# A hybrid attention layer on one NeuronCore: 166 more entries in a list that reorders the planned instructions

## The chip, the cores and the metric

The kernel runs on one core of a Trainium2 chip. Its engines, as the profile names them, are PE (TensorE, matmuls and transposes; its weight loads have a row PEld), DVE (VectorE), ACT (ScalarE), POOL (GpSimd) and SP (SyncE, which here issues every DMA). Each engine works through its own instructions in order; an instruction waits where it needs data that another engine or a transfer has not delivered. The metric is the device time of one execution in microseconds.

## What is computed

One layer of a streaming encoder, for 1024 prompt tokens and 32 sample tokens with shared weights, all in float32:

```python
def rmsnorm(x, g):
    x32 = x.astype(jnp.float32)
    y = x32 * lax.rsqrt(jnp.mean(x32 * x32, axis=-1, keepdims=True) + RMS_EPS)
    return (y * g.astype(jnp.float32)).astype(x.dtype)

def in_proj(h, g_pre, w_in):                     # w_in: 1024 x 4096
    u = rmsnorm(h, g_pre) @ w_in
    qa, ka, va, ga, qb, kb, vb, gb = jnp.split(u, SPLIT_IDX, axis=-1)
    ...

def band_attention(q, k, v, q_pos, k_pos, bias_table):     # "A", 8 heads x 64
    s = jnp.einsum('bqhd,bkhd->bhqk', q, k).astype(jnp.float32) * ATTN_SCALE
    rel = jnp.clip(k_pos[None, :] - q_pos[:, None], -REL_CLIP, REL_CLIP) + REL_CLIP
    s = s + bias_table[:, rel].astype(jnp.float32)[None]
    ...                                          # own 64-frame chunk and the 8 before it
    w = jax.nn.softmax(s, axis=-1).astype(v.dtype)
    return jnp.einsum('bhqk,bkhd->bqhd', w, v)

def stick_breaking(q, k, v, q_pos, k_pos):       # "B", 8 heads x 64
    z = jnp.einsum('bqhd,bkhd->bhqk', q, k).astype(jnp.float32) * ATTN_SCALE
    causal = (k_pos[None, :] < q_pos[:, None])[None, None]
    log_beta = jax.nn.log_sigmoid(z)
    log_1m = jnp.where(causal, jax.nn.log_sigmoid(-z), 0.0)
    after = lax.cumsum(log_1m, axis=3, reverse=True) - log_1m
    w = jnp.where(causal, jnp.exp(log_beta + after), 0.0).astype(v.dtype)
    return jnp.einsum('bhqk,bkhd->bqhd', w, v)

def finish(h, oa, ga, ob, gb, w_out, g_post, p, w_ple, w_ple_gate):
    y = jnp.concatenate([oa * jax.nn.silu(ga), ob * jax.nn.silu(gb)], axis=-1) @ w_out
    h = h + rmsnorm(y, g_post)
    return h + jax.nn.sigmoid(h @ w_ple_gate) * (p @ w_ple)
```

The sample tokens attend to cached keys and values of 512 earlier positions too. Outputs are the two results, and the new keys and values of both groups.

## The kernel before

**Arithmetic.** Every float32 operand of a matmul is split into a high part (`...h`, a cast to fp32r) and a low part (`...l`, the rest), and a product is three or four matmuls of such parts. The casts are ACT's, the subtractions DVE's or POOL's.

**Stages.** At the start, the small product `p @ w_ple` (class `Ple`: tiles `pp`, `wpr`, `php`, `ple`) fills PE while x is normed and transposed (`ptx`, `hnh`, `hnl`). Then the projection columns are made in pairs of heads (`mm_kA`, `mm_qA`, ...; weights `wr` split into `wh`, `wl`), woven (`weave`, L1352) with the attention of the pair before: pairs A0, B0, A1, B1, ... each of two heads. `A20` is pair 2 of A, head 0. Gates `gA` and `gB` follow, and at the end the products with `w_out` and `w_ple_gate`, seven block products each instead of eight, which need sums of weight blocks.

**Attention of one head.** `scores` (L915) makes eight query blocks of scores (`SA`, `SB`). For B, ACT takes the sigmoid into `om`, DVE scans along it, and POOL subtracts neighbours into `be`, the weights. For A, DVE adds the bias (`om`), and ACT takes the exponential into `be`. `weights_t` (L963) turns the weights: early blocks by PE transposes (`ptwA`, `ptwB`), blocks 4 to 7 by a DVE transpose in 32 x 32 squares and a round trip through DRAM, a store `swapA<-om` and a load `be<-swapA`. The result is split into `wTh` and `wTl`, and `values` (L1011) multiplies by the values `v2A`, `v2B` into `PVA`, `PVB`, which become `otA`, `otB` and are stored to `o_dr`. The values themselves take such a round trip too (`stvA<-swapA`, then `vtA` and `v2A`, `values_out`, L766). `om` and `be` are rings (`Arena`, L232): a new tile waits until all readers of the old one in its place are done, the stores among them.

**Weight sums.** `sum_weights` (L1390) loads four quarter blocks of `w_out` (tiles `oB`) or the gate's weight (`gB`), subtracts and adds halves of them on POOL, and stores the sums (`sum_dro`, `sum_drg`) for the last stage. They are spread over the attention of pairs A0, B0 and A2, B2.

**What sets the order.** No operation is issued as it is written. A `Recorder` collects 9,413 operations, 7,493 of them instructions and the rest (`CTL`) allocations of tiles. `order` (L402) plans them with a list scheduler and its own table of costs, improves the plan in 42 passes, and hands the best plan to `settle` (L421), which applies the list `MOVES` (L44) to it. `emit` (L531) then issues them in that order, all from L541, so each line of the profile has L541 and tiles tell the operations apart. The order in which an engine meets its instructions is this list, and SP's DMAs are part of it.

An entry `(i, j)` takes the operation at place i and puts it at place j, which is earlier. What it depends on between j and i goes ahead of it in the old order; on every engine but its own the order stays.

```python
        for i, j in MOVES:
            x = ops[i]
            need, engines, ahead, behind = set(x.after), {x.eng}, [], []
            for o in reversed(ops[j:i]):
                if o in need or (o.eng in engines and o.eng != x.eng):
                    assert o.eng != x.eng
                    ahead.append(o)
                    need |= o.after
                    if o.eng != "CTL":
                        engines.add(o.eng)
                else:
                    behind.append(o)
            ops[j:i + 1] = ahead[::-1] + [x] + behind[::-1]
```

Entries are applied one after another, so a later entry's places are those of the list that the earlier ones have left.

Of the kernel before, what the change touches and what calls it, by code (L numbers as in the profile page):

```python
# [57 lines left out]
    (5444, 5437), (6840, 6823), (5445, 5438), (6861, 6825), (696, 695), (2421, 2418), (2244, 2243), (6823, 6819), (4946, 4929), (1132, 1128),  # L58
    (4715, 4714), (1118, 1108), (2021, 1989), (1063, 1055), (725, 713), (748, 726), (1008, 1002), (2176, 2169), (3344, 3337), (2855, 2845), (3213, 3209),
    (331, 323), (1566, 1563), (1011, 1003), (2520, 2512), (6405, 6400), (8654, 8642), (6230, 6225), (6755, 6742), (3470, 3468), (3081, 3057),  # L60
    (7388, 7378), (7065, 7064), (2559, 2539), (4169, 4164), (4264, 4262), (3630, 3605), (3749, 3736), (6063, 6045),
)
PASSES, SPREAD = 42, 400

# [1912 lines left out]
```

## Time and profile before

| | before |
|---|---|
| time, median of 3 runs (range) | 772.1 us (771.61 to 772.69) |
| the profiled execution's own time | 772.48 us |
| its span, first to last instruction | 770.7 us |
| busy PE / DVE / ACT / POOL | 759.4 / 582.4 / 490.9 / 462.1 us |
| mean granted TensorE clock | 0.998 |
| HBM read / written | 107.62 / 65.30 MB, 224 GB/s over the span |

A row of the timeline gives start and length in us, engine, line, operation, output and inputs, shape and count, and in brackets how long the engine had been idle and what ended that. Rows that follow each other with the same names are merged (x2). A row of waits gives the total, the number and the longest of them. A row of the chain gives start, length and what ran, or what transfer was in flight. A row of windows gives the stretch, its length, the busy time of PE, PEld, DVE, ACT and POOL with their instructions, the granted clock, and the DMA engines' share and GB/s. PE's matmuls are pipelined, so its busy time overstates its work a little and hides the shortest waits.

### The profile page before, as it was taken

The numbers are of one execution on the slowest core, as the hardware profiler recorded it, in microseconds if no ns is written. First come the engines' busy times: TensorE is split into PE (matmuls) and PEld (weight loads), VectorE is DVE, ScalarE is ACT, GpSimd is POOL, SyncE is SP. The second block draws the span as 40 slices with busy tenths as digits, with TensorE's granted clock in tenths as the row PEclk, the third lists the DMA queues.
The fourth block names the chain that finished last, engine by engine and source line by source line (L and its number), as shares of the span: only waits on it lengthen the run. The fifth ranks groups of instructions, "written<-read, shape, count | busy, mean of one in ns | idle before, by whom it ended". The sixth has DMA issues, their size and how long they took to land.

```text
span 770.7 us, 13667 instructions
## 1 busy us (share of the span) xinstructions
PE 759.4 (99%) x4422; PEld 703.0 (91%) x4422; DVE 582.4 (76%) x1025; ACT 490.9 (64%) x995; POOL 462.1 (60%) x525
## 2 busy tenths in 40 slices
PE   8999999999999999999999999999999999999997
PEld 7999989999999999999999999999998877888786
DVE  6726879898799888978898899875563578587665
ACT  5736785666686657875677785633447967774551
POOL 6615637883344546556883336788453769898443
PEclk9999999999999999999999999999999999999999
DMA  8519999878976649999689779977687859879854
GB/s 277 169 36 271 264 279 301 233 232 266 250 218 190 184 130 276 260 273 294 183 247 289 180 209 294 273 221 207 197 276 252 281 155 337 274 251 337 272 184 137
DMA packets 184825, 182.24 MB, mean 236 GB/s; under 512 B 42177, under 2 KB 139497, under 8 KB 184754
## 3 DMA queue, kind: packets, MB, share of 16 engines
q1 hardware_dynamic: 184754, 181.37, 78.2%
q8 instruction: 35, 0.57, 0.3%
q14 instruction: 36, 0.29, 0.1%
HBM read 107.62 MB, written 65.30 MB: 224 GB/s over the span
## 4 chain that ended last, share of the span: by engine, by line
PE 88%; DMA 5%; ACT 3%; DVE 2%; SPq 1%; issue 0%; POOL 0%; ACTq 0%; DVEq 0%; POOLq 0%
PE mm_qA L541 6%; PE mm_vA L541 6%; PE mm_gA L541 6%; PE mm_gB L541 6%; PE mm_kA L541 6%; PE mm_kB L541 5%; PE mm_qB L541 4%; PE PVB L541 4%; PE SB L541 4%; PE mm_vB L541 3%; PE ple L541 3%; PE PVA L541 3%; PE SA L541 3%; PE g1P L541 3%; PE o3P L541 3%; PE o1P L541 3%
## 5 line engine op out<-in xcount | busy, mean ns | idle before, releaser
L541 POOL TENSOR_TENSOR be<-om 128x128 f32<-128x128 f32 (+7 forms) x64 | 80.4, 1261 | 52.3 <-DVE om L541 22.1
L541 DVE TENSOR_TENSOR_SCAN om<-om,SB 128x384 f32<-128x384 f32 (+5 forms) x96 | 94.4, 998 | 7.0 <-ACT om L541 4.1
L541 DVE TENSOR_TENSOR wTl<-be,wTh 128x640 fp32r<-128x640 f32 (+2 forms) x56 | 65.0, 1166 | 5.6 <-ACT wTh L541 5.5
L541 ACT ACTIVATE om<-SB 128x384 f32<-128x384 f32 (+5 forms) x96 | 44.6, 491 | 29.7 <-PE SB L541 15.3
L541 ACT ACTIVATE be<-om,statA 128x640 f32<-128x640 f32 (+3 forms) x64 | 46.4, 729 | 14.4 <-DVE statA L541 7.0
L541 DVE STREAM_TRANSPOSE om<-be 128x640 f32<-128x640 f32 (+2 forms) x56 | 49.6, 892 | 3.2 <-ACT be L541 2.4
L541 ACT CAST wTh<-be 128x640 fp32r<-128x640 f32 (+2 forms) x56 | 43.2, 774 | 11.0 <-DMA be<-swapA 7.8
L541 DVE CUSTOM_DVE_ANT_0 om<-SA,biasA 128x320 f32<-128x320 f32 (+3 forms) x64 | 29.9, 484 | 8.8 <-PE SA L541 7.5
L541 POOL TENSOR_TENSOR gB<-gB,gB 128x256 f32<-128x256 f32 x32 | 26.5, 848 | 12.6 <-DMA gB<-in_w_ple_gate_dram 6.3
L541 ACT CAST wTh<-ptwB 128x512 fp32r<-128x512 f32 (+3 forms) x48 | 22.0, 481 | 18.3 <-PE ptwB L541 12.7
L541 PE MATMUL SB<-klB,LB 128*128 128x384 f32 (+5 forms) x96 | 32.9, 347 | 0.0
L541 PE MATMUL SB<-kdB,LB 128*128 128x384 f32 (+5 forms) x96 | 32.6, 344 | 0.2 <-DVE om L541 0.2
L541 POOL TENSOR_TENSOR oB<-oB,oB 128x256 f32<-128x256 f32 x32 | 24.3, 780 | 12.4 <-DMA oB<-in_w_out_dram 10.5
L541 DVE TENSOR_TENSOR wTl<-ptwB,wTh 128x512 fp32r<-128x512 f32 (+3 forms) x48 | 25.6, 544 | 7.9 <-PE PVB L541 5.0
L541 DVE TENSOR_TENSOR SB<-SB,maskb 128x128 f32<-128x128 f32 x64 | 17.9, 289 | 15.9 <-PE SB L541 15.4
L541 POOL TENSOR_TENSOR sggA<-sggA,oggA 128x352 f32<-128x352 f32 x24 | 26.3, 1099 | 6.0 <-DVE sggA L541 5.5
L541 PE MATMUL SA<-klA,LA 128*128 128x320 f32 (+2 forms) x96 | 29.5, 318 | 0.0
L541 PE MATMUL SA<-kdA,LA 128*128 128x320 f32 (+2 forms) x96 | 29.3, 316 | 0.0
L541 POOL TENSOR_TENSOR klB<-stkB,kdB 64x1024 fp32r<-64x1024 f32 x8 | 19.2, 2400 | 9.6 <-ACT kdB L541 8.8
L541 POOL TENSOR_TENSOR klA<-stkA,kdA 64x1024 fp32r<-64x1024 f32 x8 | 20.1, 2510 | 7.8 <-ACT kdA L541 7.1
L541 PE MATMUL ptwB<-ident,be 128*128 128x128 f32 x144 | 21.8, 274 | 2.8 <-POOL be L541 1.4
L541 POOL TENSOR_TENSOR h<-h,x 128x512 f32<-128x512 f32 (+1 forms) x18 | 23.1, 1293 | 1.5 <-DVE h L541 1.4
(683 smaller groups left out, 2581.4 us busy)
## 6 DMA issues: line engine op xcount, KB each, us to landing
swapA<-om SPq DMA_DIRECT2D x32, 320.0 KB, 3.8
be<-swapA SPq DMA_DIRECT2D x32, 320.0 KB, 4.6
oB<-in_w_out_dram SPq DMA_DIRECT2D x16, 256.0 KB, 4.0
sum_dro<-oB SPq DMA_DIRECT2D x16, 256.0 KB, 4.1
gB<-in_w_ple_gate_dram SPq DMA_DIRECT2D x16, 256.0 KB, 4.1
sum_drg<-gB SPq DMA_DIRECT2D x16, 256.0 KB, 3.8
x<-in_x_prompt_dram SPq DMA_DIRECT2D x16, 256.0 KB, 5.0
turned<-hs SPq DMA_DIRECT2D x16, 256.0 KB, 5.1
```

Of the source, the lines that this page charges most:

```text
L541: getattr(getattr(tc.nc, o.what[0]), o.what[1])(*args, **kw)
```

## The change

The list `MOVES` gets 166 more entries behind the ones that are there. No operation is added, removed or resized, and nothing else differs. Followed through the order one after another, 94 of the entries move a DMA on SP, 25 an instruction of DVE, 22 of ACT, 14 of POOL and 11 of PE. 113 of them pass one instruction of their own engine, none more than six. In the end 120 of SP's 734 DMAs stand at another place of SP's order, by seven places at most; 50 of 925 on DVE, 38 of 892 on ACT, 27 of 520 on POOL and 25 of 4,422 on PE, by five places at most.

At the places that the prediction speaks of, in the times of the execution profiled before:

- SP at 1 us: the second half of `pp` and `grow` ahead of `wpr_0`. ACT: `php` ahead of the cast of `wpr_0`.
- SP at 93 to 103 us: the store `swapA<-om` of block 4 of A01 and four loads of biases change places with loads of weights `wr_qA` and key stores. At 106 to 108 us: the store of block 5 goes ahead of a load for the sums, the store of block 6 goes behind the store of block 7 and the first load `be<-swapA`. At 113 to 116 us: the load `oB` for the next sum goes behind the loads `be<-swapA` of blocks 6 and 7.
- POOL at 111 to 113 us: `be` of blocks 0 and 1 of B00 each go ahead of half a weight sum `oB`.
- ACT at 307 to 310 us: `be` of block 6 of A20, two casts `wTh` and the copy `otB` go ahead of the copies `vtA` and `v2A`.
- SP at 329 to 339 us: three loads of biases and a copy of keys go behind three loads of `gB`, a load of `wr_vA`, the load `be<-swapA` of block 4 of A21 and the stores of blocks 5 to 7.
- POOL at 344 to 348 us: `be` of block 3 of B20 goes ahead of two halves of sums `gB` and two memsets of `om`.

```diff
--- before.py
+++ after.py
@@ -58,7 +58,24 @@
     (5444, 5437), (6840, 6823), (5445, 5438), (6861, 6825), (696, 695), (2421, 2418), (2244, 2243), (6823, 6819), (4946, 4929), (1132, 1128),
     (4715, 4714), (1118, 1108), (2021, 1989), (1063, 1055), (725, 713), (748, 726), (1008, 1002), (2176, 2169), (3344, 3337), (2855, 2845), (3213, 3209),
     (331, 323), (1566, 1563), (1011, 1003), (2520, 2512), (6405, 6400), (8654, 8642), (6230, 6225), (6755, 6742), (3470, 3468), (3081, 3057),
-    (7388, 7378), (7065, 7064), (2559, 2539), (4169, 4164), (4264, 4262), (3630, 3605), (3749, 3736), (6063, 6045),
+    (7388, 7378), (7065, 7064), (2559, 2539), (4169, 4164), (4264, 4262), (3630, 3605), (3749, 3736), (6063, 6045), (88, 83), (3945, 3921), (4466, 4460),
+    (3937, 3924), (1278, 1246), (3960, 3949), (5541, 5537), (1034, 1024), (2066, 2050), (7065, 7064), (5596, 5593), (209, 204), (4474, 4471),
+    (4286, 4266), (6366, 6363), (6257, 6238), (6194, 6182), (4268, 4263), (4477, 4465), (1345, 1325), (2225, 2212), (5427, 5419), (275, 233),
+    (3839, 3821), (1149, 1130), (3968, 3912), (5511, 5492), (1114, 1090), (4612, 4606), (120, 118), (1290, 1284), (4727, 4715), (4465, 4449),
+    (1124, 1106), (6101, 6094), (4636, 4632), (4298, 4269), (2463, 2453), (6045, 6044), (6201, 6189), (1368, 1328), (3686, 3684), (94, 84), (4171, 4157),
+    (1394, 1370), (356, 322), (4268, 4267), (4262, 4261), (2538, 2522), (1365, 1358), (4784, 4775), (5957, 5950), (6332, 6307), (4305, 4271),
+    (4838, 4775), (2742, 2741), (9084, 9075), (4270, 4268), (4606, 4601), (6367, 6364), (4607, 4602), (2567, 2546), (6179, 6177), (4778, 4769),
+    (3913, 3912), (1388, 1370), (2521, 2513), (4454, 4437), (1398, 1389), (6570, 6554), (1405, 1390), (6039, 6028), (4142, 4136), (364, 339),
+    (4271, 4270), (4306, 4272), (1138, 1131), (6001, 5978), (4332, 4278), (5275, 5274), (1131, 1106), (4732, 4716), (6243, 6233), (3370, 3364),
+    (1091, 1072), (4269, 4267), (4514, 4504), (4285, 4271), (1115, 1073), (5135, 5118), (1116, 1114), (4499, 4476), (6183, 6182), (2424, 2419),
+    (4771, 4770), (1248, 1161), (4632, 4619), (1083, 1080), (4270, 4269), (946, 938), (6192, 6178), (4345, 4286), (1112, 1110), (3992, 3982),
+    (4206, 4201), (6655, 6654), (6656, 6653), (1114, 1111), (4033, 4023), (1132, 1117), (6639, 6630), (1324, 1303), (5581, 5579), (5995, 5989),
+    (6368, 6365), (5391, 5384), (4234, 4225), (4740, 4739), (5446, 5435), (5458, 5420), (4261, 4246), (4262, 4258), (5592, 5580), (2250, 2231),
+    (4498, 4492), (1312, 1303), (4644, 4620), (5019, 4980), (4213, 4180), (3822, 3821), (4268, 4261), (6031, 5989), (4354, 4291), (3950, 3927),
+    (1410, 1409), (2245, 2244), (1196, 1156), (2540, 2538), (323, 322), (1200, 1197), (4268, 4263), (4280, 4279), (243, 238), (324, 323), (6654, 6645),
+    (2368, 2357), (4195, 4180), (3046, 3020), (3720, 3714), (2029, 1989), (2332, 2317), (1133, 1118), (1107, 1072), (1575, 1574), (4046, 4035),
+    (2500, 2481), (7323, 7306), (1384, 1334), (4024, 4023), (2426, 2420), (3980, 3976), (3997, 3982), (754, 730), (1211, 1195), (4091, 4085),
+    (1143, 1118),
 )
 PASSES, SPREAD = 42, 400
```

## The prediction

> **What bounds the kernel now.** The page comes first: engine times, chain, then who waited for whom.
>
> ```profile
> span 770.7 us, 13667 instructions
> PE 759.4 (99%) x4422; PEld 703.0 (91%) x4422; DVE 582.4 (76%) x1025; ACT 490.9 (64%) x995; POOL 462.1 (60%) x525
> PEclk9999999999999999999999999999999999999999
> PE 88%; DMA 5%; ACT 3%; DVE 2%; SPq 1%; issue 0%; POOL 0%; ACTq 0%; DVEq 0%; POOLq 0%
> ```
>
> TensorE (PE) is the bound: busy for 759.4 of 770.7 us and 88% of the chain. No entry of the change adds, removes or resizes an instruction, so its busy work stays; all that a new order can win is the time in which PE stands. The view of waits, for PE alone, has it whole:
>
> ```profile
> PE ptwB L541 <- POOL be L541: 1.4, 1, 1.4
> PE ptwB L541 <- POOL sumsA L541: 1.4, 1, 1.4
> PE idle L541 <- DVE still L541: 1.3, 1, 1.3
> PE ptp L541 <- DMA pp<-in_p_prompt_dram: 0.7, 1, 0.7
> PE ptwA L541 <- DVE wTl L541: 0.6, 1, 0.6
> PE PVA L541 <- ACT wTh L541: 0.3, 1, 0.3
> PE SB L541 <- DVE om L541: 0.2, 1, 0.2
> ```
>
> Each row is one wait: its total equals its longest. The `idle` row lies ahead of the first matmul and no entry reaches it. The other six sum to 4.6 us, 3.9 without the start. That is about the ceiling of this change. So the question for each wait is whether the entries near it shorten it, and what comes late next. 108 of the 166 entries concern four stretches: 34 lie at 75 to 118 us, 14 at 296 to 315, 35 at 315 to 350, 25 at 350 to 455.
>
> **The change part by part.** *The wait at 112.0 us.* Timelines of PE, POOL and SP:
>
> ```profile
> 112.03 0.33 PE L541 MATMUL ptwB<-ident,be 128*128 128x128 f32 x1 [1.43 <-POOL be L541]
> 108.44 0.10 POOL L541 MEMSET om<- 128x1 f32 x1 [2.90 <-DVE otA L541]
> 110.90 0.72 POOL L541 TENSOR_TENSOR oB<-oB,oB 128x256 f32<-128x256 f32 x1 [2.36 <-DMA oB<-in_w_out_dram]
> 111.58 0.40 POOL L541 TENSOR_TENSOR be<-om 128x128 f32<-128x128 f32 x1
> 112.67 0.61 POOL L541 TENSOR_TENSOR be<-om 128x256 f32<-128x256 f32 x1
> ```
>
> PE transposes the 128x128 `be` that POOL makes at 111.58. POOL is in order, and ahead of that `be` stands half a weight sum (`oB`) that waits 2.36 us for a load. The entries put this `be` ahead of the sum, and the second `be` (112.67) ahead of the sum's other half. The first can then start when the memset of 108.44 is done, by 108.6: 3 us early, so the 1.4 goes. Next is the second `be`: it stands behind the first half sum, whose load holds the same turn on SP. It starts at 110.90 + 0.72 = 111.6 and ends at 112.2; PE, 1.4 us earlier, asks for it at about 112. I leave 0.2 and take -1.2; bounds 0 and -1.4.
>
> *The wait at 123.1 us* (the 0.3 of the waits), from the chain and PE's timeline:
>
> ```profile
> 116.56 5.70 DMA be<-swapA
> 123.06 0.68 PE L541 MATMUL PVA<-wTh,v2A 128*128 128x512 f32 x2 [0.25 <-ACT wTh L541]
> ```
>
> `wTh` needs a load of `be` that took 5.70 us. SP gets to it earlier: a load for the sums goes behind it. But PE comes 1.2 us earlier as well, and one of the four stores whose data this load reads back moves two places later. I cost it at nothing, bounds +1.2 (the load doesn't move, PE does) and -0.3.
>
> *The waits at 309.0 us.* ACT, DVE and PE:
>
> ```profile
> 307.18 1.05 ACT L541 COPY vtA<-stvA 128x1024 f32<-128x1024 f32 x1 [2.22 <-DMA stvA<-swapA]
> 308.14 0.53 ACT L541 CAST wTh<-ptwA 128x256 fp32r<-128x256 f32 x2
> 309.81 0.90 ACT L541 ACTIVATE be<-om,statA 128x640 f32<-128x640 f32 x1
> 308.70 0.29 DVE L541 TENSOR_TENSOR wTl<-ptwA,wTh 128x128 fp32r<-128x128 f32 x1 [1.29 <-ACT wTh L541]
> 309.05 0.55 PE L541 MATMUL ptwA<-ident,be 128*128 128x128 f32 x3 [0.58 <-DVE wTl L541]
> ```
>
> ACT stands 2.22 us before the `vtA` copy, which waits for a transfer, and behind it are two casts (0.53) that free the bank PE waits for. The entries put the `be` of 309.81 (0.90), both casts and then the `otB` copy ahead of `vtA`. ACT is free from 307.18 - 2.22 = 304.96; with 0.90 and 0.53 the casts end near 306.4 in place of 308.7, so DVE and PE have 2 us to spare: -0.6. `vtA` itself waits for its transfer as before. Next in line on ACT are the casts of the later banks, and these come sooner too, by the 0.90 taken out ahead of them. Bounds 0 and -0.6.
>
> *The waits at 344.6 and 348.2 us.* PE, DVE, POOL, the chain and SP:
>
> ```profile
> 344.61 0.45 PE L541 MATMUL SB<-kdB,LB 128*128 128x384 f32 x1 [0.24 <-DVE om L541]
> 348.22 0.55 PE L541 MATMUL ptwB<-ident,be 128*128 128x128 f32 x3 [1.37 <-POOL sumsA L541]
> 343.28 1.27 DVE L541 TENSOR_TENSOR_SCAN om<-om,SB 128x512 f32<-128x512 f32 x1
> 343.42 1.42 POOL L541 TENSOR_TENSOR gB<-gB,gB 128x256 f32<-128x256 f32 x2
> 346.36 0.13 POOL L541 MEMSET om<- 128x1 f32 x2 [1.52 <-DMA o_dr<-otA]
> 346.45 0.72 POOL L541 TENSOR_TENSOR gB<-gB,gB 128x256 f32<-128x256 f32 x1
> 347.14 1.02 POOL L541 TENSOR_TENSOR be<-om 128x512 f32<-128x512 f32 x1
> 335.84 5.92 DMA be<-swapA
> 337.08 1.53 SPq L541 DMA_DIRECT2D swapA<-om  x3
> ```
>
> PE waits for the 128x512 `be` of 347.14. Its input is ready when the scan ends, at 344.55; it stands behind two memsets, which wait 1.52 us for stores to land, and behind the second `gB` of the pair at 343.42 and the one at 346.45. The entries put it ahead of all of these, right behind the first `gB` of the pair, done by 344.2: it can start at 344.6 and end at 345.6, against 348.2. On SP the load at 335.84 and the first store at 337.08 go three places forward, past loads of biases and a copy of the next head's keys; with 1.53 / 3 = 0.5 us a place that is 1.5 us. The scan stands behind that load's consumers on DVE, so it comes earlier too, and with it the 0.2. I take -1.4 - 0.2 = -1.6; bounds 0 and -1.6. The biases moved back, seven places at most (some 3.5 us), belong to the sample attention of the next pair.
>
> *The start.* On SP the second half of `pp` and `grow` go ahead of the weights `wpr_0`; on ACT `php` goes ahead of their cast:
>
> ```profile
> 1.24 0.45 SPq L541 DMA_DIRECT2D wpr_0True<-in_w_ple_dram  x1
> 4.69 0.62 ACT L541 CAST wph0True<-wpr_0True 128x512 fp32r<-128x512 f32 x1 [2.69 <-DMA wpr_0True<-in_w_ple_dram]
> 5.82 1.12 PE L541 MATMUL ptp<-ident,pp 128*128 128x128 f32 x4 [0.73 <-DMA pp<-in_p_prompt_dram]
> 6.58 2.91 PE L541 MATMUL ple<-wph0True,php 128*128 128x512 f32 x6
> ```
>
> The two transfers trade landings: `pp` at about 4.7 in place of 5.8, `wpr_0` at 5.8 or later, then the cast of 0.62, and `ple` can begin at 6.45 or later against 6.58. The wait moves from `ptp` to `ple`: 0, bounds -0.5 and +0.5 (two places of 0.45).
>
> *The rest.* The 25 matmuls that change places move by at most three, past ready ones: 0. The other SP swaps put swap stores and `be` reloads ahead of key outputs, which nobody reads, and sums; the DVE, ACT and POOL swaps behind 350 us lie where PE has no wait: 0, bounds ±0.5 by the size of the small rows above.
>
> Sum: -1.2 - 0.6 - 1.6 = -3.4 us, plus zeros. The profiled execution took 772.48 us, 1.8 around its span; 769.1 follows. The median shown is 772.1, 0.4 less: **768.7 us**.
>
> **The rivals.** *The transfers set the time* (A). The windows of the stretches:
>
> ```profile
> 105.00:118.00 13.00, 11.57 (x73) 11.23 (x72) 9.74 (x16) 8.82 (x19) 4.62 (x11) 1.00 0.98 305
> 296.00:315.00 19.00, 18.35 (x117) 16.90 (x116) 15.72 (x44) 13.91 (x33) 8.07 (x9) 1.00 0.99 279
> ```
>
> The last two columns are the share of the DMA engines and GB/s: at 0.98 and 0.99 nothing lands sooner by being issued sooner unless another lands later. If landings stand in absolute time, what PE wins at 112 it waits for again at the next `swapA` round trip (+0.3 grows to +1.2 at 123.1), and of the last stretch only half the POOL swap stays: -1.2 + 1.2 - 0.6 - 0.8 = -1.4, **770.7**. Against it: these transfers carry data that PE's own products feed, and so start earlier with PE.
>
> *POOL is held elsewhere* (B, slower). The load of the next weight sum goes two places back, and in POOL's order the later `be` tiles still stand behind such sums. A hold like the 2.36 of 110.90, moved to a place with less cover, costs 2.4 where 1.4 was won; at both sums' groups 2 x (2.4 - 1.4) = +2.0: **774.1**. It decides once that load lands over 1.4 us after POOL has got to the sum. Against it: the load moves by only about 1 us.
>
> *The change doesn't do what it says* (C): the landings differ so much between executions that the waits of this one are not those of the next; the zeros decide and it stays at **772.1**. For it: one execution is profiled. Against: the runs shown spread over 1.1 us alone, less than one of the two 1.4 us waits.
>
> [...]
>
> **How the numbers follow.** The sum as it stands, within 767.0 to 770.5 (two of the small terms or half of one large one missing): 0.60. A: 0.18. B: 0.10. C: 0.06. D: 0.06. A measurement of this kernel tells about 0.2%, 1.5 us, from no change. Faster by more (under 770.6): the sum and D, 0.66, and a part of A, 0.04: 0.70. Within: the rest of A, C and a little of B: 0.21. Slower: 0.09. Low end 766.8: all six waits gone, 772.1 - 4.6 = 767.5, less a part of D. High end 772.8: it takes in A and C and leaves out B.
>
> **What the profile after would show.** Right: PE's waits for POOL in the `ptwB` rows (1.4 and 1.4) and for DVE in `ptwA` gone, and the 128x128 `be` at 108 to 109 us right behind the memset. The start: a wait of `ple` on the cast of `wpr_0` in place of `ptp` on `pp`. A: waits of `PVA` or `SB` on `wTh` or `om`, over 1 us. B: POOL idle on `oB` or `gB` with PE's `ptw` waiting. The forecast is wrong if PE's waits in the page's view sum to over 3 us without the `idle` row; then the new rows name the queue that paid.

## The result and the profile after

| | before | after |
|---|---|---|
| median of 8 executions each, one chip | 771.62 us (770.21 to 772.69) | 767.95 us (765.39 to 771.88) |
| ratio after / before, 95% interval | | 0.9956 (0.9934 to 0.9977) |
| the profiled execution, its span | 772.48, 770.7 us | 769.36, 767.6 us |

The change wins 0.44%, 3.7 us. The page of the changed kernel, the three lines that answer to those of before:

```profile
span 767.6 us, 13677 instructions
PE 758.8 (99%) x4422; PEld 703.3 (92%) x4422; DVE 580.3 (76%) x1025; ACT 490.4 (64%) x995; POOL 462.7 (60%) x525
PE 94%; DMA 3%; ACT 1%; DVE 1%; issue 0%; SPq 0%; ACTq 0%
```

PE's busy time is the same within 0.6 us and its share of the chain rises from 88% to 94%: what went is standing time. PE's waits in the changed kernel:

```profile
PE idle L558 <- DVE still L558: 1.3, 1, 1.3
PE PVA L558 <- ACT wTh L558: 0.9, 1, 0.9
PE ple L558 <- ACT wph0True L558: 0.7, 1, 0.7
PE SB L558 <- DVE LB L558: 0.5, 1, 0.5
PE ptksB L558 <- DMA be<-in_cache_b_k_dram: 0.5, 1, 0.5
```

Without the `idle` row that is 2.6 us against 4.6. All six waits of the first trace are gone from their places; the start's has moved from `ptp` to `ple`, and three new ones stand at 217.8 us (`SB`), 349.2 (`PVA`) and 469.4 (`ptksB`). The 128x128 `be` now stands right behind POOL's memset and ahead of the sum, in POOL's timeline:

```profile
107.02 0.39 POOL L558 TENSOR_TENSOR be<-om 128x128 f32<-128x128 f32 x1 [0.51 <-DVE om L558]
108.89 0.73 POOL L558 TENSOR_TENSOR oB<-oB,oB 128x256 f32<-128x256 f32 x1 [1.48 <-DMA oB<-in_w_out_dram]
```

So far it looks like the forecast come true. The experiments show that the time was right, and that much of the credit went to the wrong entries.

### The profile page after: what moved, and what is told of

Read it like the earlier page. It is cut to its first block, busy times and chain, and to the rows that moved or that the text cites. A ratio compares the mean times of both kernels' runs of the same rounds, so it can differ in the third digit from the quotient of the medians.

```text
span 767.6 us, 13677 instructions
## 1 busy us (share of the span) xinstructions
PE 758.8 (99%) x4422; PEld 703.3 (92%) x4422; DVE 580.3 (76%) x1025; ACT 490.4 (64%) x995; POOL 462.7 (60%) x525
## 4 chain that ended last, share of the span: by engine, by line
PE 94%; DMA 3%; ACT 1%; DVE 1%; issue 0%; SPq 0%; ACTq 0%
PE mm_qA L558 6%; PE mm_vA L558 6%; PE mm_kB L558 6%; PE mm_gB L558 6%; PE mm_qB L558 6%; PE mm_kA L558 6%; PE mm_gA L558 5%; PE mm_vB L558 5%; PE PVB L558 4%; PE SB L558 4%; PE SA L558 4%; PE ple L558 3%; PE PVA L558 3%; PE o3P L558 3%; PE g1P L558 3%; PE o1P L558 3%
## 5 line engine op out<-in xcount | busy, mean ns | idle before, releaser
L558 DVE TENSOR_TENSOR wTl<-be,wTh 128x640 fp32r<-128x640 f32 (+2 forms) x56 | 61.1, 1098 | 6.3 <-ACT wTh L558 5.9
L558 POOL TENSOR_TENSOR oB<-oB,oB 128x256 f32<-128x256 f32 x32 | 27.6, 886 | 12.3 <-DMA oB<-in_w_out_dram 11.4
L558 ACT CAST wTh<-ptwB 128x512 fp32r<-128x512 f32 (+3 forms) x48 | 22.2, 485 | 19.2 <-PE ptwB L558 13.7
L558 POOL TENSOR_TENSOR gB<-gB,gB 128x256 f32<-128x256 f32 x32 | 25.7, 824 | 13.7 <-DMA gB<-in_w_ple_gate_dram 7.6
L558 POOL TENSOR_TENSOR sggB<-sggB,oggB 128x352 f32<-128x352 f32 x12 | 13.2, 1100 | 15.2 <-DVE sggB L558 11.6
```

The source lines that it names most:

```text
L558: getattr(getattr(tc.nc, o.what[0]), o.what[1])(*args, **kw)
```

## The experiments

Theory 1 is the prediction's: a wait belongs to the order of the instructions, and each is won where its own cause is moved. Theory 2 is the prediction's rival A, landings in absolute time. Theory 3: the three new waits are the price of the moved transfers. Theories 4 and 5 came up on the way and are explained where they are first used. POOL's four entries are those of its 14 that move the `be` to which the prediction gave the waits of `ptwB`. Each part of the change was built from the same entries, with the places worked out anew for the list in which they then stand.

| kernel | median (range), executions | before on the same chip | ratio, 95% interval |
|---|---|---|---|
| whole change, again | 766.66 (765.55 to 768.03), 7 | 770.84, 12 | 0.9949 (0.9930 to 0.9968) |
| POOL's 4 entries alone | 770.05 (766.49 to 776.39), 12 | 770.57, 29 | 0.9995 (0.9975 to 1.0015) |
| SP's 94 alone | 769.15 (766.72 to 771.16), 12 | 770.57, 29 | 0.9974 (0.9955 to 0.9993) |
| SP's 94 alone, again | 768.99 (767.49 to 771.44), 12 | 771.59, 26 | 0.9974 (0.9956 to 0.9993) |
| all but SP's, 72 | 771.30 (767.69 to 775.25), 12 | 770.57, 29 | 1.0020 (0.9999 to 1.0041) |
| all but SP's, again | 772.48 (768.30 to 774.53), 12 | 771.59, 26 | 1.0010 (0.9989 to 1.0032) |
| all but POOL's 4 | 767.33 (765.22 to 768.76), 6 | 770.57, 29 | 0.9955 (0.9937 to 0.9973) |
| all but the start's 10 | 766.38 (765.89 to 768.23), 6 | 771.59, 26 | 0.9939 (0.9915 to 0.9962) |
| whole and 6 more on SP | 767.48 (766.71 to 771.03), 9 | 771.59, 26 | 0.9960 (0.9939 to 0.9980) |

The second table is from the traces: how much earlier (-) or later PE starts its instruction of the same number than in the first trace of the kernel before, in us, at the instructions that stand there at the times named.

| trace | 41.3 | 85.3 | 118.4 | 244.8 | 324.1 | 358.2 | 483.7 | 765.1 |
|---|---|---|---|---|---|---|---|---|
| before, second | -0.28 | -0.28 | -1.43 | -2.04 | -2.15 | -2.02 | -0.74 | -0.70 |
| before, third | -1.09 | -0.91 | -1.94 | -1.90 | -1.91 | -2.08 | -2.12 | -2.13 |
| after, first | +0.05 | +0.05 | -1.60 | -1.28 | -2.46 | -3.28 | -2.71 | -2.71 |
| after, second | -1.12 | -1.12 | -2.78 | -3.28 | -4.44 | -6.40 | -6.44 | -6.50 |
| after, third | -1.19 | -1.19 | -2.85 | -3.25 | -4.43 | -6.42 | -5.95 | -5.94 |
| POOL's 4 alone | -0.40 | -0.40 | -2.04 | -1.82 | -1.84 | -3.84 | -3.00 | -3.02 |
| SP's alone | +0.91 | +0.91 | -0.50 | -1.03 | -0.51 | -2.30 | -0.84 | -0.87 |
| SP's alone, again | +1.45 | +1.45 | -0.19 | -0.55 | -0.75 | -1.55 | -0.53 | -0.61 |
| all but SP's | +0.91 | +0.91 | -0.75 | +0.01 | -1.14 | -3.05 | -1.83 | -1.84 |
| all but SP's, again | +0.04 | +0.04 | -1.61 | -2.01 | -3.16 | -4.13 | -4.17 | -4.18 |
| all but POOL's 4 | -1.13 | -1.13 | -2.78 | -3.23 | -4.41 | -5.19 | -5.34 | -5.36 |
| all but the start's | +0.88 | +0.88 | -0.77 | -1.29 | -2.44 | -4.06 | -4.14 | -4.14 |
| whole and 6 more | -1.18 | -1.18 | -2.83 | -3.39 | -4.58 | -6.39 | -4.70 | -4.75 |

A row stays constant where PE doesn't wait (41 to 85 us, 484 to 765: within 0.2 us in every trace), so each step in a row behind 41 us is a wait that is there in one trace and not in the other. Up to 41 us PE's pace differs too (last section).

### POOL's four entries alone

```diff
+    (4477, 4464), (4464, 4449), (1394, 1370), (1364, 1356),
```

> Only the four entries that move POOL's three products `be` (beB00_0, beB00_1, beB20_3) ahead of its longer sum and of the memsets. Theory 1 (TensorE's waits add up, and each is won where its own cause is taken away): both waits of ptwB of 1.4 us go, TensorE's lead on the kernel before is about -1.4 us behind 112 us and -2.6 to -2.8 us behind 348 us, and the time is 2.0 to 2.8 us under before. Theory 2 (landings have times of their own, so whatever brings TensorE forward is given back at the next late transfer): the waits go as well, but the waits at 123.1, 309 and 344.6 us grow by what was won, and the time is less than 1 us under before. Theory 3 (the three new waits of the changed kernel, at 217.8, 349.2 and 469.4 us, are made by the moved transfers): none of the three is here, since no transfer is moved.

Both waits of `ptwB` are gone (steps of -1.64 at 85 to 118 and -2.00 at 324 to 358), but the medians differ by 0.5 us only, and 2.0 to 2.8 lies outside of the interval (1.9 us faster to 1.2 us slower). Theory 1 is wrong in its size, though in this one trace PE ends 2.1 us earlier than in the three of before on average (-3.02 against -0.94). Most of that comes from which executions were traced: this one, 769.46 us, lies 0.6 under the median of its 12, those of before, 771.5 on average, 0.9 over the 770.57 of the 29 here. A wait that the first trace of before didn't have stands in this kernel, which moves no transfer:

```profile
PE ptksB L542 <- DMA be<-in_cache_b_k_dram: 0.7, 1, 0.7
```

That is one of the three new waits of the changed kernel. So theory 3 falls for it.

### SP's 94 entries alone, and all the others alone

```diff
+    (88, 83), (1278, 1246), (5541, 5537), (1034, 1024), (7065, 7064), (4286, 4266), (6194, 6182), (4268, 4263), (1345, 1325), (5427, 5419),
...
+    (1211, 1195), (1143, 1118),
```

> Only the 94 entries on SP's list; POOL, ACT, DVE and PE keep the order of before. Theory 1: the two waits of ptwB stay at about 1.4 us, the small ones of PVA at 123.1 and SB at 344.6 us go or shrink, and the time is within 0.7 us of before. Theory 2: no change, within 0.3 us. Theory 3: the new waits at 217.8 (0.5 to 0.7 us), 349.2 (0.9) and 469.4 us (0.5) are here too, and the time is 0.5 to 1.5 us over before.

```diff
+    (3945, 3921), (4466, 4460), (3937, 3924), (3960, 3949), (2066, 2050), (5596, 5593), (209, 204), (4474, 4471), (6366, 6363),
...
+    (2332, 2317), (4046, 4035), (2500, 2481), (7323, 7306), (2426, 2420), (3980, 3976), (3997, 3982), (4091, 4085),
```

> The 72 entries on ACT, DVE, POOL and PE; SP keeps the order of before. Theory 1: the waits at 112.0, 309 and 348.2 us go, those of 0.3 and 0.4 us at 123.1 and 344.6 us may stay or grow, and the time is 2.5 to 3.5 us under before, within 0.5 us of the whole change. Theory 2: the waits at 123.1 and 344.6 us grow to about 1 us each, and the time is 1 to 2 us under before. Theory 3: the three new waits are not here, and the time is 1 us or more under that of the whole change.

No theory had it this way round: SP's entries alone win 0.26%, and the rest, with all the POOL and ACT moves to which the prediction gave 3.2 of its 3.4 us, wins nothing that shows. Both waits of `ptwB` are gone with SP's entries, though POOL keeps the order of before (-1.41 and -1.79 us in the second table). The two parts together win 3.7 to 4.2 us by the medians; singly they stand at -1.4 and +0.7.

### All but POOL's four

```diff
-    (4477, 4465), (4465, 4449), (1394, 1370), (1365, 1358),
```

(the four as the change has them; the other 162 stay.)

> The whole change without the four entries on POOL's three products `be`. Theory 1: both waits of ptwB are back with 1.2 to 1.9 us each (TensorE comes earlier to the second by what was won before it), and the time is 2.2 to 2.8 us over the whole change, 0.5 to 1 us under before. Theory 2: the waits are back, but the three new ones at 217.8, 349.2 and 469.4 us shrink by as much, and the time is within 1 us of the whole change. Theory 3: the waits are back and the three new ones stay as they are; the time is at or over that of before.

Theory 1 asked for two waits of 1.2 us and more and a time near before's. There is neither: 0.9955, as the whole change. At the second place `PVA` waits 0.98 us at 347.3 in place of `ptwB`, as it does in the changed kernel's first trace. For the first place, POOL's timeline of this kernel, PE's and SP's show why:

```profile
107.30 0.74 POOL L559 TENSOR_TENSOR oB<-oB,oB 128x256 f32<-128x256 f32 x1 [2.31 <-DMA oB<-in_w_out_dram]
107.99 0.40 POOL L559 TENSOR_TENSOR be<-om 128x128 f32<-128x128 f32 x1
```

```profile
109.30 0.28 PE L559 MATMUL ptwB<-ident,be 128*128 128x128 f32 x1
```

```profile
102.83 1.29 SPq L559 DMA_DIRECT2D oB<-in_w_out_dram  x1
```

The same load in the first trace of the kernel before:

```profile
105.76 1.06 SPq L541 DMA_DIRECT2D oB<-in_w_out_dram  x2
```

The `be` still stands behind the sum, and the sum still waits 2.31 us for its load. But the load lands sooner: SP issues it (the first of a pair) at 102.83 and the sum starts at 107.30, 4.5 us later; that time is 4.9 to 6.0 us in the six traces with SP's order of before and 3.8 to 4.5 in the eight with SP's entries. The `be` is done at 108.4, 0.9 us before PE asks. Two cures for one wait: either is enough, and the second adds little.

How far ahead of PE the load is issued counts as much. In the first trace of before PE would have come to this `ptwB` 4.8 us after the issue (112.03 - 1.43 - 105.76), in the second and third 6.8 and 6.0 us after it, and in the three traces with SP's entries and POOL's old order 5.4 to 6.5. So the 1.4 us of the first trace is also a late issue: SP had stood 1.1 us for a landing of `wr_qA` just before. The load that took longest, 6.0 us in the second trace, cost PE only 0.3.

### Both kernels again

> The kernel before, unchanged, for a second trace of it. In the three kernels tried with SP's moves or POOL's moves alone, other waits stood at other places, so the question is what belongs to the order and what to the one execution. Theory 1 (waits belong to the order of the instructions): the two waits of ptwB at 112 and 348 us are here again with 1.2 to 1.7 us each, and TensorE's waits without the idle row are 3 to 5 us in all. Theory 4 (the landings of one execution set them): one or both are missing or under 0.5 us, and waits of 0.5 us and more stand where the first trace had none, as those of SsA at 425 or of ptksB at 469 us.

> A third trace of the kernel before. Theory 1: as in the first two, both waits of ptwB with 1.2 to 1.7 us. Theory 4: the places and sizes of the waits differ from those of the other two traces by more than 1 us in all.

The kernel before, second and third trace, PE's waits:

```profile
PE ple L541 <- ACT wph1True L541: 1.4, 1, 1.4
PE idle L541 <- DVE still L541: 1.3, 1, 1.3
PE ptp L541 <- DMA pp<-in_p_prompt_dram: 1.0, 1, 1.0
PE ptksB L541 <- DVE om L541: 0.9, 1, 0.9
PE PVA L541 <- ACT wTh L541: 0.8, 1, 0.8
PE ptwA L541 <- DVE wTl L541: 0.5, 1, 0.5
PE SB L541 <- DVE om L541: 0.4, 1, 0.4
PE ptwB L541 <- POOL be L541: 0.3, 1, 0.3
```

```profile
PE ptwB L541 <- POOL sumsA L541: 1.4, 1, 1.4
PE idle L541 <- DVE still L541: 1.3, 1, 1.3
PE ptp L541 <- DMA pp<-in_p_prompt_dram: 1.0, 1, 1.0
PE ple L541 <- ACT wph1True L541: 0.5, 1, 0.5
PE ptwA L541 <- DVE wTl L541: 0.6, 1, 0.6
PE PVA L541 <- ACT wTh L541: 0.3, 1, 0.3
```

Theory 4 holds for most of them. The `ptwB` wait at 112 us is 1.4, 0.3 and none in three executions of one program, that at 348 us 1.4, none and 1.4. In the second trace the latter is replaced by a wait of `PVA` at 350.5, of 0.8: PE stands a little later, on `wTh`. `ptksB` waits once in three. What is in all three is less: `ptwA` at 307 to 309 us with 0.6, 0.5 and 0.6, and `ptp` at the start with 0.7, 1.0 and 1.0.

> The changed kernel, unchanged, for a second trace and for more times beside those of the kernel before on one chip. Theory 1: the three new waits (SB at 217.8, PVA at 349.2, ptksB at 469.4 us) are here again within 0.3 us of 0.7, 1.1 and 0.6 us. Theory 4: at least one is missing, and another place has one. Both: no wait of ptwB at 110 or 346 us, since its `be` stands ahead of POOL's sum; the time 2.5 to 4 us under before.

> A third trace of the changed kernel. Theory 1: the same three waits. Theory 4: others; the sum behind the first 40 us between 0 and 3 us.

The changed kernel, second and third trace:

```profile
PE idle L558 <- DVE still L558: 1.3, 1, 1.3
PE ple L558 <- ACT wph0True L558: 1.2, 1, 1.2
```

```profile
PE idle L558 <- DVE still L558: 1.3, 1, 1.3
PE ple L558 <- ACT wph0True L558: 1.1, 1, 1.1
PE SA L558 <- DVE statA L558: 0.3, 1, 0.3
```

None of the three new waits is here: they were the first execution's. This is theory 4 again. The sums without `idle` are 2.6, 1.2 and 1.4 us against 4.6, 5.3 and 3.8 before. Over three traces each, (13.7 - 5.2) / 3 = 2.8 us of waits go on average, and the first trace of the changed kernel showed it at its worst.

### The two halves again

> SP's 94 entries alone, a second time, with a new trace. So far: the waits at 110 to 124 and 338 to 351 us (1.6 to 3.9 us in the three traces of the kernel before) were 0.26 us in this kernel's first trace, though POOL's order is that of before, and its time was 1.4 us under before. Theory 5 (SP's moves carry the gain in these two stretches, by loads and swaps that are issued earlier; POOL's moves only do the same over again): those stretches hold under 0.6 us again, the wait of ptwA at 309 us stands (0.6 to 1.3, it hangs on DVE and PE), and the time is 1.5 to 2.5 us under before. Theory 1 as predicted (SP's moves worth 0 with 0.5 us either way): the first trace was a chance, ptwB waits 1 us or more at 112 or 348 us, time within 0.5 us of before.

> The 72 entries on ACT, DVE, POOL and PE alone, a second time. So far: 0.7 us over before by the medians though its trace had 1.9 us less of waits. Theory 5: the wait at 123 us stands (0.4 to 1.2 us, it hangs on a swap that SP issues late), those of ptwB and ptwA are gone, and the time is 0 to 2 us under before. Theory 1 as predicted: 2.5 to 3.5 us under before.

The ratios repeat, 0.9974 and 1.0010. For SP's entries theory 5 is right in the time and half right in the places: the wait at 112 us is gone, but the stretch of 338 to 351 us holds a wait of `ptwB` (0.3) and one of `PVA` (0.6), and `ptwA` waits 0.3, less than expected. With the others alone the median is 0.9 us over before, where theory 5 asked for 0 to 2 us under, and the wait at 123 us that it wanted to stand was 1.1 us in the first trace and isn't in the second. What can hold SP's entries alone back, 2 us short of the whole, is seen in their second trace, PE's waits and ACT's timeline. Both of their traced executions (771.16 and 771.44 us) are the slowest of their 12, so this is what can stand there and not the usual case:

```profile
PE ple L552 <- ACT php L552: 2.1, 1, 2.1
...
PE SsA L552 <- ACT QsA L552: 0.7, 1, 0.7
```

```profile
6.30 0.62 ACT L552 CAST wph0True<-wpr_0True 128x512 fp32r<-128x512 f32 x1 [4.30 <-DMA wpr_0True<-in_w_ple_dram]
6.82 1.07 ACT L552 CAST php<-ptp 128x512 fp32r<-128x512 f32 x2
```

SP's entries put the load of `wpr_0` behind `pp`. Without ACT's entry, both `php` casts stay behind the cast that waits for this load: ACT stands 4.30 us, until 6.30, though PE's last `ptp` ends at 5.4. PE comes to 41 us 0.91 and 1.45 us later than in the first trace of before. The whole change comes 0.05 us later in the one of its traces that has the same 0.43 us between matmuls at the start (last section), and 1.1 to 1.2 us earlier in the other two. Then `ptwA` at 309 us stays, since ACT's `vtA` is not moved (steps of +0.52 and -0.20 at 245 to 324 us, against -1.15 to -1.19 in every trace with ACT's entries). And `SsA` waits for `QsA` at 425 us in both traces, a copy that an ACT entry moves forward. All but SP's, which have that entry, wait there too, 0.6 us in one of two traces; with both parts the wait is in none of six. So at the start and at 425 us entries on two queues look as if they only win together; no run has such a pair by itself.

Why the others alone win nothing in time is open. In their traces PE ends earlier than in the first of before (by 1.84 and 4.18 us; SP's alone by 0.87 and 0.61), so the traces rank the two halves the other way round than the times do. But their profiled executions, 770.63 and 768.30 us, lie under the medians of their 12, and the second is the fastest of them. What the other executions waited for was not traced. The finding that SP's entries carry the gain rests on the times of 24 executions each.

### The start

```diff
-    (88, 83), (209, 204), (275, 233), (120, 118), (94, 84), (356, 322), (364, 339), (323, 322), (243, 238), (324, 323),
```

> The whole change without the ten entries of the first 35 us (the swaps of pp, grow and wpr_0, of php and wph, and POOL's there). As predicted (start worth 0): the time is within 0.5 us of the whole change's, and the first wait is that of ptp on the load of pp with 0.7 to 1.0 us in place of ple's. If the start is worth something: TensorE comes to its 50th instruction about 0.5 us later than in the changed kernel's traces (13.4 to 14.9 us), and the time is 0.5 to 1 us longer.

At 0.9939 against 0.9949 and 0.9956 for the whole, the start's entries are worth nothing that can be measured. In its one trace the wait of `ptp` is back and `ptx` waits 0.9 at 33 us, which costs 2.0 us up to 41 us against the whole change's later traces; one of the whole change's three has no such lead either. PE's 50th matmul, at 14.1 us, lies within the 13.3 to 14.8 of the whole change's three traces, not 0.5 us behind them.

### Six more moves at the three new waits

```diff
+    (6045, 6007), (4290, 4285), (4294, 4290), (4439, 4438), (4458, 4439), (2573, 2540),
```

> The whole change and six more moves on SP at the three places where the changed kernel's first trace had waits: the load KcsB1 five steps earlier (some 3 us), the two swaps swapA21_6 and swapA21_7 ahead of the load wr_vA3_1, the reloads beA21_6 and beA21_7 ahead of the load for the sum that stands before them, and rs_dr<-sumrowA10 ahead of two stores and two loads. If these waits come from late issues: none at 217.8, 349.2 or 469.4 us in its trace, and the time 0.3 to 1.5 us under the whole change's, 4.0 to 5.5 under before. If the landings of one execution set them whatever the order: one such wait in the trace or another beside it, and the time within 0.5 us of the whole change's.

The three waits are not in its trace, as in two of three without the repair, and one of 1.6 us is new. No gain: 0.9960. The load `be<-in_cache_b_k_dram` (`KcsB1`), moved six places forward, now heads SP's queue at a time when the tile that it takes is still being read. SP's waits at 455 to 467 us and its timeline:

```profile
SPq L560 <- DVE wTl L560: 2.8, 1, 2.8
SPq L560 <- DMA swapB<-vxB: 1.7, 1, 1.7
```

```profile
455.96 0.58 SPq L560 DMA_DIRECT2D wr_gA<-in_w_in_dram  x1
459.35 0.38 SPq L560 DMA_DIRECT2D be<-in_cache_b_k_dram  x1
...
461.35 0.43 SPq L560 DMA_DIRECT2D swapB<-vxB  x1
...
465.67 1.29 SPq L560 DMA_DIRECT2D stvB<-swapB  x2
```

The changed kernel's second trace, where PE and SP come to this place within 0.3 us of the same time:

```profile
458.50 0.38 SPq L558 DMA_DIRECT2D swapB<-vxB  x1
...
460.74 0.43 SPq L558 DMA_DIRECT2D be<-in_cache_b_k_dram  x1
...
461.86 1.28 SPq L558 DMA_DIRECT2D stvB<-swapB  x2
```

The load gained 1.4 us, and the cast that hangs on it (`Kh0sB`) starts at 466.23 us against 466.26: nobody needed it earlier. Behind it the store `swapB<-vxB` went from 458.50 to 461.35, and the reload that needs its landing from 461.86 to 465.67. ACT and PE paid:

```profile
470.97 1.05 ACT L560 COPY vtB<-stvB 128x1024 f32<-128x1024 f32 x1 [4.16 <-DMA stvB<-swapB]
```

```profile
473.54 0.82 PE L560 MATMUL PVB<-wTh,v2B 128*128 128x512 f32 x4 [1.63 <-DVE Kl0sB L560]
```

The whole change, with or without the ten entries of the start, POOL's four or these six, stands at 0.9939 to 0.9960; these can't be told apart.

## Why the prediction was right in the time and wrong in the credit

Forecast 768.7 us, 3.4 under before; measured 767.95, 3.7 under, and 4.2 under in the second comparison. That the sum fits is in part luck: it was priced on one trace, the longest execution of before that was traced, and its misses go both ways. The steps, by the second table: three traces of the changed kernel on average less three of before (its first row being zero).

| term | predicted | by the traces |
|---|---|---|
| start, to 85 us | 0 (+-0.5) | -0.75 - (-0.40) = -0.4 |
| 112.0 us, POOL's `be` (85 to 118) | -1.2 | -1.66 - (-0.73) = -0.9 |
| 123.1 us, `wTh` (118 to 245) | 0 | 0.0 |
| 309.0 us, ACT's casts (245 to 324) | -0.6 | -1.17 - (-0.04) = -1.1 |
| 344.6 and 348.2 us (324 to 358) | -1.6 | -1.59 - (-0.01) = -1.6 |
| behind 358 us | 0 (+-0.5) | +0.32 - (+0.42) = -0.1 |
| sum | -3.4 | -4.1 |

- **Only PE's waits can be won: right but for 0.4 us.** Behind the start PE keeps the same pace between waits in all traces (within 0.2 us over 41 to 85 and over 484 to 765 us, in the second table), and the sum of the steps, -4.1, is the gain in time within its interval. The spans of the same six traces differ by more, 4.5 us on average (the three of before, 771.5 us, lie 0.6 over the median of 75 executions, so both differences are a little large). The rest lies behind PE's last matmul:

```profile
765.06 0.29 PE L541 MATMUL g3P3b<-gB,wlS4g 128*128 128x256 f32 x1
767.05 0.42 DVE L541 TENSOR_TENSOR uu<-uu,hh 128x256 f32<-128x256 f32 x1
```

```profile
758.56 0.29 PE L558 MATMUL g3P3b<-gB,wlS4g 128*128 128x256 f32 x1
760.55 0.42 DVE L558 TENSOR_TENSOR uu<-uu,hh 128x256 f32<-128x256 f32 x1
```

From this matmul to the span's end it is 5.6 us in the first trace of before (770.7) and 5.2 in the second of the changed kernel (763.8); it is 5.6 in all six traces with SP's order of before and 5.2 in all eight with SP's entries. The last DVE instruction stands 1.99 us behind the matmul in both, so the 0.4 lies in what closes the program; its cause is open. The prediction had no term for it.

- **112.0 us: right in the place, wrong in the cause's share.** The hold was there as described, POOL's `be` behind a sum whose load is late. But in two of three executions of before it cost 0.3 us or nothing, since SP issued the load earlier ahead of PE, and with SP's entries alone the load is there 3.8 to 4.5 us after its issue in place of 4.9 to 6.0 and nothing is left to wait for. POOL's entries alone change the time by -0.5 us (interval -1.9 to +1.2), and without them the whole loses nothing that shows.
- **309.0 us: the surest term, and too small.** It is in all three traces of before and in none with ACT's entries, which were not run apart from those of DVE and PE. The row gave 0.58 for `ptwA`; the step is 1.1. By the distances between PE's starts `ptwA` lost 0.74 in the first trace, and a second stall of 0.3 at 312.9 us, of `PVA`, too short for the view of waits, comes and goes with it in every trace.
- **344.6 and 348.2 us: the size right,** 1.6. Again either cure works: steps of -2.00, -1.91 and -0.97 with POOL's entries in SP's old order, -1.79, -0.80 and -0.78 with SP's entries without POOL's four, and -0.82 to -1.99 with both. The smaller ones are traces in which `PVA` waits 0.4 to 1.0 us behind it.
- **The rest of SP at 0 (+-0.5): the step that failed.** SP's entries are worth 2.0 us alone (interval 0.5 to 3.5), and without them the other 72 win nothing. The prediction looked for causes at the engines that held PE and priced a queue's order by its 0.5 us a place. What counted instead, as far as the traces show it, is what a load or a store and reload waits behind, and how often in many executions it comes late: the load for the sum is one place where it was measured (3.8 to 4.5 us in place of 4.9 to 6.0), and 0.4 us in both traces of SP's entries alone are those behind PE's last matmul. Which other places make up the 2.0 us isn't known.
- **Rival C (the waits of this execution aren't those of the next), at 0.06, was nearly right in its premise** and wrong in its conclusion: the single waits vary by over 1 us each, yet their sum falls, from 3.8 to 5.3 us in the three traces of before to 1.2 to 2.6 in the three of the changed kernel. The prediction's argument against it, three times within 1.1 us, was too weak: 75 executions of before spread from 767.67 to 775.32.
- **Rival A** is seen in places: at 350.5 us in before's second trace and at 349.2 us in the changed kernel's first one, `PVA` waits where `ptwB` no longer does. It takes back 0.8 and 0.9 us there, and nothing in the other four traces of the two kernels; of the kernels with parts of the change, three traces have it too (0.98 without POOL's four, 0.56 in the second with SP's alone, 0.41 in the second of all but SP's). So the rival is right at this place in five of the twelve traces where the wait of `ptwB` is gone or down to 0.3 us, and wrong in the whole.
- **Rival B** did not come: in no trace of the changed kernel does PE wait for POOL.
- **Rival D** (PE's slow pace at the start ends earlier; it has 0.06 and a part of the low end): no run shows the 1.7 us put on it. What the traces show in its place: the matmuls of 512 columns start 0.43 us apart until 9.6 to 11.3 us in 6 of 14 traces and 0.23 apart from the first one in 8, with both kernels in both groups, and the changed kernel's two traces with 0.23 lead its one with 0.43 by 1.17 and 1.24 us at 41 us. So the pace is a matter of the execution more than of the change; in one trace a granted clock of 0.50 follows a wait (last section).

Not settled: why over 772 us is reached only with SP's old order, by 20 of 75 executions of before, 1 of 12 of POOL's alone and 10 of 24 of all but SP's, and by none of 61 with SP's entries. These counts show that SP's new order cuts off the long executions, but not by which waits; of the traced executions only before's first, 772.48, is that long.

## What to carry to other kernels

Where a kernel hangs on many transfers with little slack, a single trace shows which waits can happen, not which will (here one wait was 1.4 us, 0.3 and none in three traces of one program): take three before a wait is given a price, keep the ones that are in all of them, and look where the traced execution stands among the timed ones: here the slowest of one kernel's 12 was set beside the fastest of another's. A wait with two causes, an order on the engine and a late load behind it, was won by either here (the one at 112 us by -1.64 us with POOL's entries alone, -1.41 with SP's, -1.65 to -1.66 with both), so the parts of such a change don't add up. Before a load is moved forward in an in-order queue, look whether its buffer is free by then: here it wasn't, the queue stood 2.8 us, a reload behind it was issued 3.8 us later, and PE waited 1.6.

## What the runs showed of the hardware

PE's pace at the start falls in two groups. PE's timeline in the changed kernel's first and second trace:

```profile
6.61 2.93 PE L558 MATMUL ple<-wph0True,php 128*128 128x512 f32 x6 [0.67 <-ACT wph0True L558]
```

```profile
6.77 1.65 PE L558 MATMUL ple<-wph0True,php 128*128 128x512 f32 x6 [1.22 <-ACT wph0True L558]
```

In 6 of the 14 traces the matmuls of 512 columns follow each other mostly at 0.43 us until 9.6 to 11.3 us, in the other 8 at 0.23 from the first one, at 6.4 to 7.0 us. In the record one of them lasts 0.63 us at the pace of 0.43 (at 9.34 us in the changed kernel's first trace) and 0.39 at 0.23 (at 8.65 us in before's second), so its end lies behind the start of the next. Both groups hold traces of before and of after. The two rows differ by 2.93 - 1.65 = 1.28 us. In three of the traces with 0.23 a part of such a lead is given back by a wait for `wph1`: 1.4 us in before's second trace, 0.5 in its third, 1.0 without the start's entries. What decides between the two groups isn't shown. In one of the six the granted clock falls to 0.50: the second trace with SP's entries alone, 0.7 us behind a wait of PE of 2.05 us, in windows:

```profile
7.00:8.00 1.00, 0.55 (x2) 0.30 (x2) 0.57 (x1) 0.89 (x2) 1.00 (x1) 1.00 0.93 274
9.00:10.00 1.00, 1.00 (x3) 0.76 (x3) 1.00 (x2) 0.19 (x2) 0.82 (x2) 0.50 0.98 363
12.00:13.00 1.00, 1.00 (x6) 0.83 (x5) 0.00 (x0) 0.87 (x3) 1.00 (x1) 1.00 1.01 401
```

Its first two such matmuls come 0.34 and 0.39 us apart, and the 0.50 lasts from 8.1 to 11.5 us. That the wait brought it on isn't shown; the 1.4 us in before's second trace is followed by no such stretch. In the other five the view has 1.00 over the stretch of 0.43, yet the record of the full clock in their traces begins only where that stretch ends, at 9.6 to 10.7 us; in the eight others it begins at 4.2 to 6.5.

The time from the issue of one and the same load to its first reader varies by about a microsecond from one execution to the next (the load for the sum at 110 us: 5.1, 6.0 and 4.9 us in the three traces of before, where the DMA engines are 0.98, 0.91 and 0.99 busy from 105 to 118 us). That alone doesn't decide whether PE waits: the waits were 1.4, 0.3 and none, as the load was issued 4.8, 6.8 and 6.0 us before PE's turn.
